# Latent attention: rope scores with 128 rows, against rope keys kept twice and padded with zeros

## The chip, the core and the metric

The kernel runs on one core of a Trainium2 chip. The metric is the device time of one execution, in microseconds (us). The engines of the core are TensorE (PE for its matmuls, PEld for its weight loads), VectorE (DVE), ScalarE (ACT), GpSimd (POOL) and SyncE (SP), which issues most of the loads. Each works through its own queue in order and waits on semaphores for the others.

## What is computed

The reference chains two blocks over 256 tokens of 1024 features. The first has stick-breaking attention, attention to a memory and a feed-forward net; the second has a layer with latent attention and a layer with a long convolution (Hyena), each followed by a convolved feed-forward net. The change concerns the latent attention alone:

```
def mla_mixer(x, cos, sin, w_in, g_q, w_uq, g_kv, w_ukv, w_o):
    h = x @ w_in
    c_q, c_kv, k_rope = jnp.split(h, [Q_LORA_RANK, Q_LORA_RANK + KV_LORA_RANK], axis=-1)
    q = (rms_norm(c_q, g_q) @ w_uq).reshape(b, s, MLA_HEADS, QK_NOPE_DIM + QK_ROPE_DIM)
    q_nope = q[..., :QK_NOPE_DIM]
    q_rope = apply_rope(q[..., QK_NOPE_DIM:], cos[:, :, None], sin[:, :, None])
    k_rope = apply_rope(k_rope, cos, sin)
    ...
        sc = (jnp.einsum('bqhd,bkhd->bhqk', qn, k_nope)
              + jnp.einsum('bqhr,bkr->bhqk', qr, k_rope))
        p = jax.nn.softmax(sc.astype(jnp.float32) * scale, axis=-1).astype(v.dtype)
        return jnp.einsum('bhqk,bkhd->bqhd', p, v)
```

There are 8 heads. A head's query and key have 128 features without position ("nope") and 64 with rotary position ("rope"). The rope key is one for all heads.

## The kernel before

Activations are kept with features on the partitions (rows) and the 256 tokens along the free dimension. Each fp32 product is made of three matmuls of split operands: a high part and a low part, hi x hi, lo x hi, hi x lo (`mm3`, lines 106 to 109; `gemm_b` at L102 for projections). A split is a copy on ACT (L69) and a subtract on DVE (L70). Weights come through a raw tile (`wraw`) and are split into `whi` and `wlo`.

The latent attention goes like this. `c_mm` and `first_pair` give the compressed queries, keys and the rope key (in rows 0 to 63 and once more in rows 64 to 127, since the host repeats its columns). `qr` matmuls give the rope queries, two heads on the 128 rows of a tile: four tiles of `rope_in`, and the rope key as the fifth. GpSimd's queue copies `rope_in` with its halves swapped to `rope_sw`. `rotate(i)` multiplies by the cosine and sine tables, adds, and splits tile i into `rope_h` and `rope_l`.

Eight `Latent` heads then run through `pipeline`: `scores`, `turn`, `values`, each head a step behind the one before, with the projections of head h + 2 (`mla_proj`: `qn`, `kn`), further rotations and the first output products (`u_wo`, tile `acc`) as fillers. For each of two blocks of 128 queries, `scores` makes three matmuls over the 128 nope rows and three over the 64 rope rows of its head (`r`: rows 0 to 63 for an even head, 64 to 127 for an odd one), all into one PSUM bank `z`. Heads 0 to 4 take the two banks `z300` and `z301` in turn, so head 2 has to wait until head 0's exponentials are read; the others take `z3` banks of the common pool. Then DVE takes the row maximum (`sm_nm`, L262), ACT the exponentials (`sm_p`, L270), DVE the reciprocal and the scaling (L273, L275); PE transposes (`pt`, L282), ACT copies (`sm_pt`, L284), PE multiplies with the values (`o`, L733), and the result is split into `oT`.

The order on each engine is set by the tile framework's scheduler, not by the text: it takes instructions of different heads as its own estimates let them come ready. Buffers (three of each of `qn` and `kn`, three raw tiles, five split pairs) set when loads and splits can go ahead.

Of the kernel before, what the change touches and what calls it, by code (L numbers as in the profile page):

```python
# [9 lines left out]
F32 = mybir.dt.float32  # L10
F32R = mybir.dt.float32r
# [7 lines left out]
P = 128  # L19
S = 256  # L20
# [25 lines left out]
def block_kernel(ctx, tc, A, out, taps=None):  # L46
    nc = tc.nc
# [10 lines left out]
    def bank(name="ps"):  # L58
        return psp.tile([P, 512], F32, name=name, tag="ps")

    def acc_bank(b, h, name="acc"):
        return accp.tile([P, 512], F32, name=f"{name}{b}{h}", tag=f"acc{b}{h}")
# [5 lines left out]
    def split(hi, lo, src, eng=nc.vector):  # L68
        nc.scalar.activation(hi, src, AF.Copy)  # L69
        eng.tensor_tensor(lo, src, hi.bitcast(F32), op=ALU.subtract)  # L70
# [34 lines left out]
    def mm3(ps, a, m, start, stop):  # L105
        (ah, al), (mh, ml) = a, m
        nc.tensor.matmul(ps, ah, mh, start=start, stop=False)  # L107
        nc.tensor.matmul(ps, al, mh, start=False, stop=False)  # L108
        nc.tensor.matmul(ps, ah, ml, start=False, stop=stop)  # L109
# [149 lines left out]
    def softmax(pool, z, scale, scale_ap):  # L259
        z = z.rearrange("p (b s) -> p b s", b=2)  # L260
        nm = small.tile([P, 2], F32, name="sm_nm", tag="sm_nm")
        nc.vector.tensor_reduce(nm, z, axis=AX.X, op=ALU.max, negate=True)  # L262
        if scale_ap is None:
            nc.vector.tensor_scalar(nm, nm, scale, None, op0=ALU.mult)
        else:
            nc.vector.tensor_tensor(nm, nm, scale_ap, op=ALU.mult)
        p = pool.tile([P, 2, S], F32, name="sm_p", tag="sm_p", bufs=2)
        sm = small.tile([P, 2], F32, name="sm_s", tag="sm_s")
        for b in range(2):
            nc.scalar.activation(p[:, b, :], z[:, b, :], AF.Exp, bias=nm[:, b:b + 1],  # L270
                                 scale=scale if scale_ap is None else scale_ap[:, b:b + 1],
                                 accum_out=sm[:, b:b + 1])
        nc.vector.reciprocal(sm, sm)  # L273
        for b in range(2):
            nc.vector.tensor_scalar(p[:, b, :], p[:, b, :], sm[:, b:b + 1], None, op0=ALU.mult)  # L275
        return p
# [42 lines left out]
    for k in range(KT):  # L319
# [3 lines left out]
        for b in range(2):  # L323
            tb = slice(b * P, (b + 1) * P)
# [75 lines left out]
    class Stick:  # L400
# [5 lines left out]
        def scores(self):  # L406
            q, k = qk["q", self.pair], keys[self.pair % 2]
            late, early = acc_bank(0, 0, "z"), acc_bank(0, 1, "z")
            mm3(early[:, :S], [t[:, :P] for t in q], [t[:, :, :P] for t in k], True, True)
            mm3(late, [t[:, P:] for t in q], [t for t in k], True, True)  # L410
            ze = early[:, :S].rearrange("p (h s) -> p h s", h=2)
            zl = late.rearrange("p (h g s) -> p h g s", h=2, g=2)
            stay = stays[self.pair % 2]
            w = p1.tile([P, 2, 3, P], F32, name="sb_w", tag="sb_w", bufs=2)
            for t, sc in ((stay, -0.125), (w, 0.125)):
                nc.scalar.activation(t[:, :, 0, :P], ze, AF.Sigmoid, scale=sc)
                nc.scalar.activation(t[:, :, 1:, :P], zl, AF.Sigmoid, scale=sc)
            later = p1.tile([P, 2, 3, 129], F32, name="sb_later", tag="sb_later", bufs=2)
            flat = [t.rearrange("p h g s -> p (h g s)")[:, ::-1] for t in (later, stay, reset)]
            nc.vector.tensor_tensor_scan(flat[0], flat[1], flat[2], 0.0, op0=ALU.mult, op1=ALU.max)  # L420
            nc.vector.tensor_tensor(w, w, later[:, :, :, 1:], op=ALU.mult)
            self.w = w
# [174 lines left out]
    p3 = ph.enter_context(tc.tile_pool(name="p3", bufs=1))  # L597
# [6 lines left out]
    sq = p3.tile([P, S], F32, name="sq")  # L604
    rope_in = p3.tile([P, 5, S], F32, name="rope_in")
    rope_sw = p3.tile([P, 5, S], F32, name="rope_sw")
    rope_h = p3.tile([P, 5, S], F32R, name="rope_h")
    rope_l = p3.tile([P, 5, S], F32R, name="rope_l")

    def c_mm(nt):  # L610
        w = weights(A["mla_w_in"][nt - 4])
# [22 lines left out]
    def rms_scales():  # L634

        for b in range(2):
            for dst, cs in ((rkv, slice(384, 512)), (rq, slice(0, 384))):
                junk = p3.tile([P, 384], F32, name="junk", tag="junk", bufs=2)
                nc.scalar.activation(junk[:, :cs.stop - cs.start], utok[:, b, cs], AF.Square,
                                     accum_out=dst[:, b:b + 1])  # L640
        ps = bank("ss")
        for b in range(2):
            nc.tensor.matmul(ps[:, b:b + 1], sq[:, b * P:(b + 1) * P], ones, start=True, stop=True)
        nc.vector.tensor_tensor(rkv, rkv, ps[:, :2], op=ALU.add)
        for dst, n in ((rkv, 256), (rq, 384)):
            nc.vector.tensor_scalar(dst, dst, 1.0 / n, RMS_EPS, op0=ALU.mult, op1=ALU.add)
            nc.gpsimd.tensor_tensor(dst, dst, mhalf, op=ALU.pow)
        nc.vector.tensor_scalar(rq, rq, 192.0 ** -0.5, None, op0=ALU.mult)
# [3 lines left out]
    for i in range(2):  # L652
        w = weights(A["w_uq_r"][i])
        for j in range(2):
            ps = bank("qr")
            gemm_b(ps[:, :S], w, j * 384, cq, 3)
            nc.scalar.activation(rope_in[:, 2 * i + j, :], ps[:, :S], AF.Copy)
    rms_scales()
    for q in range(4):
        s0 = (q ^ 1) * 32  # L660
# [40 lines left out]
    def rotate(i):  # L701
        nc.vector.tensor_tensor(rope_in[:, i, :], rope_in[:, i, :], cosT, op=ALU.mult)
        nc.vector.tensor_tensor(rope_sw[:, i, :], rope_sw[:, i, :], sinT, op=ALU.mult)
        nc.vector.tensor_tensor(rope_in[:, i, :], rope_in[:, i, :], rope_sw[:, i, :], op=ALU.add)
        split(rope_h[:, i, :], rope_l[:, i, :], rope_in[:, i, :])

    rotate(4)
    rotate(0)

    class Latent:  # L710
# [2 lines left out]

        def scores(self):
            h = self.h
            r = slice(64 * (h % 2), 64 * (h % 2) + 64)
            z = acc_bank(0, h % 2, "z3") if self.own else bank("z3")
            for b in range(2):
                tb = slice(b * P, (b + 1) * P)
                zb = z[:, b * S:(b + 1) * S]  # L720
                mm3(zb, [t[:, tb] for t in qn[h]], kn[h], True, False)
                mm3(zb, [t[r, h // 2, tb] for t in (rope_h, rope_l)],
                    [t[r, 4, :] for t in (rope_h, rope_l)], False, True)
            self.p = softmax(p3, z, None, rq)

        def turn(self):
# [17 lines left out]
    for i in range(1, 4):  # L744
        filler[2 * i - 2].append((rotate, i))
# [448 lines left out]
```

## Time and profile before

| | us |
|---|---|
| median of three runs | 989.87 |
| the three runs | 989.59, 989.87, 994.86 |
| profiled execution | 988.41 |
| its span, first to last instruction | 986.6 |
| busy: PE, PEld, DVE, ACT, POOL | 946.4, 841.1, 760.4, 524.5, 123.3 |

A span of 986.6 us in an execution of 988.41 leaves 1.8 us around it. Matmuls are listed with their fill and drain, so that neighbours overlap: how fast PE goes is seen from the distance between two starts, not from a duration. "64*128" behind a matmul is its form on the array, rows by columns; "128*128" is the whole. A row of the timeline gathers neighbours of one kind (x3), and its duration runs to the end of the last. In brackets stands the idle time before it and who ended it.

### The profile page before, as it was taken

How to read it: one execution, taken by the hardware profiler on the slowest of the kernel's cores; microseconds unless marked ns; L12 is line 12 of the kernel's file. 1: busy time of each engine (PE TensorE's matmuls, PEld its weight loads, DVE VectorE, ACT ScalarE, POOL GpSimd, SP SyncE). 2: the span in 40 equal slices, each digit the busy share in tenths (PEclk: the TensorE clock that was granted, in tenths of full speed). 3: DMA queues.
4: the chain of work that ended last, by engine and by line, in shares of the span. 5: the costliest groups of instructions: out<-in, count | busy, mean ns of one | idle time of the engine just before them, and what ended most of it. 6: DMA issues, size and time to landing. Idle time of an engine off the chain costs nothing.

```text
span 986.6 us, 15543 instructions
## 1 busy us (share of the span) xinstructions
PE 946.4 (96%) x6020; PEld 841.1 (85%) x6020; DVE 760.4 (77%) x1177; ACT 524.5 (53%) x859; POOL 123.3 (12%) x78
## 2 busy tenths in 40 slices
PE   9999999999999999999999999998879899999996
PEld 7889789888998888888899999788867789999995
DVE  6776678666557777779889887869998778777776
ACT  5676526445445576556666665345453346555551
POOL 0000000000000110011311211177453000000000
PEclk9999999999999999999999999999999899999999
DMA  7744436656565543466545556443222455555551
GB/s 242 278 170 129 154 122 221 178 190 179 183 192 187 173 128 107 149 244 210 196 164 184 171 170 220 132 160 106 98 86 86 171 192 193 179 185 185 181 191 43
DMA packets 48921, 165.97 MB, mean 168 GB/s; under 512 B 5995, under 2 KB 6860, under 8 KB 48720
## 3 DMA queue, kind: packets, MB, share of 16 engines
q1 hardware_dynamic: 48656, 164.34, 50.5%
q8 instruction: 47, 0.77, 0.3%
q0 software_dynamic: 192, 0.66, 0.2%
q14 instruction: 26, 0.21, 0.1%
HBM read 163.27 MB, written 1.05 MB: 167 GB/s over the span
## 4 chain that ended last, share of the span: by engine, by line
PE 76%; DVE 13%; DMA 5%; ACT 3%; issue 2%; POOL 0%; SPq 0%; DVEq 0%; ACTq 0%
PE up L102 30%; PE acc L108 8%; PE acc L107 8%; PE acc L109 8%; PE f L189 5%; PE proj L102 2%; DVE wlo L70 2%; PE z L107 1%; DMA wraw<-w_qk 1%; DVE yl L70 1%; DVE spec_q L956 1%; ACT whi L69 1%; DVE spec_q L955 1%; PE qn L102 1%; DMA wraw<-w_v 1%
## 5 line engine op out<-in xcount | busy, mean ns | idle before, releaser
L70 DVE TENSOR_TENSOR wlo<-wraw,whi 128x1024 fp32r<-128x1024 f32 (+1 forms) x246 | 300.6, 1225 | 71.2 <-ACT whi L69 70.9
L69 ACT ACTIVATE whi<-wraw 128x1024 fp32r<-128x1024 f32 (+1 forms) x270 | 281.0, 1045 | 113.3 <-PE acc L108 54.3
L102 PE MATMUL up<-xh,whi 128*128 128x256 f32 x864 | 122.0, 283 | 1.3 <-DVE t L763 1.3
L102 PEld LDWEIGHTS up<-xh,whi 128*128 128x128 f32 x864 | 115.3, 191 | 8.3 <-ACT whi L69 1.6
L102 PE MATMUL up<-xh,wlo 128*128 128x256 f32 x864 | 121.3, 283 | 0.0
L102 PE MATMUL up<-xl,whi 128*128 128x256 f32 x864 | 121.3, 283 | 0.0
L108 PE MATMUL acc<-whi,hl 128*128 128x512 f32 x304 | 119.6, 394 | 1.5 <-DVE hl L70 1.5
L109 PE MATMUL acc<-wlo,hh 128*128 128x512 f32 x304 | 119.6, 395 | 0.0
L107 PE MATMUL acc<-whi,hh 128*128 128x512 f32 x304 | 119.3, 394 | 0.0
L102 PEld LDWEIGHTS up<-xl,whi 128*128 128x128 f32 x864 | 111.5, 192 | 0.0
L102 PEld LDWEIGHTS up<-xh,wlo 128*128 128x128 f32 x864 | 111.4, 192 | 0.0
L156 POOL TENSOR_TENSOR ln_rs<-ln_rs,mhalf 128x1 f32<-128x1 f32 x12 | 11.7, 971 | 629.1 <-DVE ln_rs L155 629.1
L760 ACT ACTIVATE t<-up,wc 128x256 f32<-128x256 f32 x80 | 37.8, 474 | 94.8 <-PE up L102 94.7
L761 DVE SCALAR_TENSOR_TENSOR t<-up,wc,t 128x255 f32<-128x255 f32 x80 | 38.2, 479 | 51.4 <-ACT t L760 51.3
L108 PEld LDWEIGHTS acc<-whi,hl 128*128 128x128 f32 x304 | 57.1, 188 | 12.9 <-DVE hl L70 2.5
L109 PEld LDWEIGHTS acc<-wlo,hh 128*128 128x128 f32 x304 | 57.1, 188 | 12.7
L107 PEld LDWEIGHTS acc<-whi,hh 128*128 128x128 f32 x304 | 57.6, 189 | 10.9 <-ACT hh L69 0.6
L70 POOL TENSOR_TENSOR wlo<-wraw,whi 128x1024 fp32r<-128x1024 f32 x24 | 59.5, 2497 | 54.8 <-ACT whi L69 54.7
L763 DVE SCALAR_TENSOR_TENSOR t<-up,wc,t 128x255 f32<-128x255 f32 x80 | 38.3, 480 | 2.1
L524 ACT ACTIVATE h<-up 128x256 f32<-128x256 f32 x28 | 10.8, 385 | 54.7 <-PE up L102 51.5
L525 DVE TENSOR_TENSOR h<-h 128x256 f32<-128x256 f32 x32 | 13.5, 424 | 27.0 <-ACT h L524 26.4
L829 POOL TENSOR_TENSOR Kf<-f_eo 128x512 f32<-128x512 f32 x16 | 23.0, 1460 | 63.5 <-ACT f_eo L826 63.5
(411 smaller groups left out, 1684.6 us busy)
## 6 DMA issues: line engine op xcount, KB each, us to landing
wraw<-ffn_w_up SPq DMA_DIRECT2D x80, 512.0 KB, 3.5
wraw<-ffn_w_down SPq DMA_DIRECT2D x44, 512.0 KB, 3.5
wraw<-w_down SPq DMA_DIRECT2D x32, 512.0 KB, 3.7
wraw<-w_up SPq DMA_DIRECT2D x28, 512.0 KB, 3.6
wraw<-hy_w_in SPq DMA_DIRECT2D x20, 512.0 KB, 3.3
wraw<-w_qk SPq DMA_DIRECT2D x14, 512.0 KB, 4.6
wraw<-w_out SPq DMA_DIRECT2D x8, 512.0 KB, 3.5
wraw<-mla_w_o SPq DMA_DIRECT2D x8, 512.0 KB, 3.3
```

The costliest lines, as they stand in the source:

```text
L69: nc.scalar.activation(hi, src, AF.Copy)
L70: eng.tensor_tensor(lo, src, hi.bitcast(F32), op=ALU.subtract)
L102: nc.tensor.matmul(ps, a[:, off + k * P:off + (k + 1) * P], m[:, k, :], start=i == 0, stop=i == len(seq) - 1)
L107: nc.tensor.matmul(ps, ah, mh, start=start, stop=False)
L108: nc.tensor.matmul(ps, al, mh, start=False, stop=False)
L109: nc.tensor.matmul(ps, ah, ml, start=False, stop=stop)
L189: nc.tensor.matmul(ps, x[xi][:, k, tb], ws[k // 2][wi][:, o:o + 512], start=i == 0, stop=i == len(seq) - 1)
L525: nc.vector.tensor_tensor(h, h, h, op=ALU.mult)
L760: norm["act"] = nc.scalar.activation(dst, ps, AF.Copy, scale=w3[:, 1:2])
L761: nc.vector.scalar_tensor_tensor(dst[:, 1:], ps[:, :S - 1], w3[:, 0:1], dst[:, 1:], op0=ALU.mult, op1=ALU.add)
L763: norm["dve"] = nc.vector.scalar_tensor_tensor(dst[:, :S - 1], ps[:, 1:S], w3[:, 2:3], dst[:, :S - 1], op0=ALU.mult, op1=ALU.add)
L829: nc.gpsimd.tensor_tensor(Kf[:, o, i, j, cs], eo[0], eo[1], op=op)
```

## The change

The five tiles of split rope rows become four (the queries), and the rope key gets tiles of its own, `krh` and `krl` (`kr`), of 128 x 2 x 256: in half 0 the key stands in rows 0 to 63 with zeros in rows 64 to 127, in half 1 the other way round. Four memsets write the zeros, at the start of the stage. For tile 4 `rotate` splits the rope key in two pieces of 64 rows. `scores` then multiplies all 128 rows of a query tile, which holds two heads, with the half that belongs to the head: the other head's rows meet zeros. `junk` has one buffer instead of two.

```
     rope_in = p3.tile([P, 5, S], F32, name="rope_in")
     rope_sw = p3.tile([P, 5, S], F32, name="rope_sw")
-    rope_h = p3.tile([P, 5, S], F32R, name="rope_h")
-    rope_l = p3.tile([P, 5, S], F32R, name="rope_l")
+    rope_h = p3.tile([P, 4, S], F32R, name="rope_h")
+    rope_l = p3.tile([P, 4, S], F32R, name="rope_l")
+
+    kr = [p3.tile([P, 2, S], F32R, name=f"kr{t}") for t in "hl"]
+    for t in kr:
+        nc.vector.memset(t[64:, 0, :].bitcast(F32), 0.0)
+        nc.vector.memset(t[:64, 1, :].bitcast(F32), 0.0)
...
-                junk = p3.tile([P, 384], F32, name="junk", tag="junk", bufs=2)
+                junk = p3.tile([P, 384], F32, name="junk", tag="junk")
...
-        split(rope_h[:, i, :], rope_l[:, i, :], rope_in[:, i, :])
+        if i < 4:
+            split(rope_h[:, i, :], rope_l[:, i, :], rope_in[:, i, :])
+            return
+        for j in range(2):
+            r = slice(64 * j, 64 * j + 64)
+            split(kr[0][r, j, :], kr[1][r, j, :], rope_in[r, i, :])
...
             h = self.h
-            r = slice(64 * (h % 2), 64 * (h % 2) + 64)
             z = acc_bank(0, h % 2, "z3") if self.own else bank("z3")
...
                 mm3(zb, [t[:, tb] for t in qn[h]], kn[h], True, False)
-                mm3(zb, [t[r, h // 2, tb] for t in (rope_h, rope_l)],
-                    [t[r, 4, :] for t in (rope_h, rope_l)], False, True)
+                mm3(zb, [t[:, h // 2, tb] for t in (rope_h, rope_l)], [t[:, h % 2, :] for t in kr], False, True)
```

The number of score matmuls stays. The scheduler also orders some work differently. On PE, between the scores of head 3 (`z_3915` before, `z_3923` now) and those of head 4 (`z_3996`, `z_4004`), stood the first five score matmuls of head 5 (`z_4060`, `z_4068`). Before:

```order
L109 MATMUL z_3915<-rope_l,rope_h 128x256
L107 MATMUL z_4060<-knh,qnh 128x256
L108 MATMUL z_4060<-knh,qnl 128x256
L109 MATMUL z_4060<-knl,qnh 128x256
L107 MATMUL z_4060<-rope_h 128x256
L108 MATMUL z_4060<-rope_h,rope_l 128x256
L107 MATMUL z_3996<-knh,qnh 128x256
```

Now, at the same place on PE:

```order
L109 MATMUL z_3923<-krl,rope_h 128x256
L107 MATMUL z_4068<-knh,qnh 128x256
L107 MATMUL z_4004<-knh,qnh 128x256
L108 MATMUL z_4004<-knh,qnl 128x256
L109 MATMUL z_4004<-knl,qnh 128x256
L107 MATMUL z_4004<-krh,rope_h 128x256
```

One of head 5's matmuls is left ahead of head 4's; the other four moved behind them. On DVE, at the start of the stage, stand the splits of weights (`wlo`), the scales of the queries (`rq`) and the low parts of the compressed vectors (`cl`). Before:

```order
L70 TENSOR_TENSOR wlo<-wraw,whi 128x768 x2
L646 TENSOR_SCALAR rq<-rq 128x2
L648 TENSOR_SCALAR rq<-rq 128x2
L70 TENSOR_TENSOR wlo<-wraw,whi 128x768
L619 SCALAR_TENSOR_TENSOR cl<-c,gqk,ch 128x256
```

Now, at the same place on DVE:

```order
L70 TENSOR_TENSOR wlo<-wraw,whi 128x768 x2
L612 MEMSET krh 64x256
L613 MEMSET krh 64x256
L612 MEMSET krl 64x256
L613 MEMSET krl 64x256
L70 TENSOR_TENSOR wlo<-wraw,whi 128x768
L651 TENSOR_SCALAR rq<-rq 128x2
L653 TENSOR_SCALAR rq<-rq 128x2
L624 SCALAR_TENSOR_TENSOR cl<-c,gqk,ch 128x256
```

The memsets stand behind the second split of 768 columns, and the third such split moved ahead of the two operations on rq.

## Rows read from the trace of the kernel before

**Rows 1.** The page, part 1: busy us (share of the span) x instructions.
```profile
PE 946.4 (96%) x6020; PEld 841.1 (85%) x6020; DVE 760.4 (77%) x1177; ACT 524.5 (53%) x859; POOL 123.3 (12%) x78
```
**Rows 2.** Busy by stretch: us; PE, PEld, DVE, ACT, POOL; clock, DMA share, GB/s.
```profile
358.50:391.20 32.70, 32.70 (x196) 26.00 (x195) 26.89 (x74) 22.72 (x58) 0.00 (x0) 1.00 0.23 81
391.20:416.00 24.80, 24.76 (x115) 19.93 (x115) 18.70 (x29) 14.21 (x21) 0.94 (x1) 1.00 0.51 171
```
**Rows 3.** Timeline, PE and PEld, head 1's scores: start us, us, instruction.
```profile
361.14 0.28 PE L108 MATMUL z<-knh,qnl 128*128 128x256 f32 x1
361.15 0.19 PEld L109 LDWEIGHTS z<-knl,qnh 128*128 128x128 f32 x1
361.26 0.27 PE L109 MATMUL z<-knl,qnh 128*128 128x256 f32 x1
361.46 0.18 PEld L107 LDWEIGHTS z<-rope_h 64*128 64x128 f32 x1
361.46 0.38 PE L107 MATMUL z<-rope_h 64*128 64x256 f32 x1
361.69 0.28 PE L108 MATMUL z<-rope_h,rope_l 64*128 64x256 f32 x1
361.81 0.28 PE L109 MATMUL z<-rope_l,rope_h 64*128 64x256 f32 x1
362.02 0.39 PE L102 MATMUL kn<-ch,whi 128*128 128x256 f32 x1
...
362.24 0.40 PE L102 MATMUL kn<-ch,wlo 128*128 128x256 f32 x2
```
**Rows 4.** Timeline, PE: projections in one form.
```profile
362.71 0.51 PE L102 MATMUL qn<-ch,whi 128*128 128x256 f32 x3
...
363.77 0.40 PE L102 MATMUL kn<-ch,whi 128*128 128x256 f32 x2
```
**Rows 5.** Timeline, PE: the first and the last run of 64 rows.
```profile
358.53 0.39 PE L107 MATMUL z<-rope_h 64*128 64x256 f32 x2
...
390.67 0.38 PE L107 MATMUL z<-rope_h 64*128 64x256 f32 x1
```
**Rows 6.** Timeline, ACT and PE: ahead of head 2's scores.
```profile
361.63 0.39 ACT L69 ACTIVATE qnh<-qn 128x256 fp32r<-128x256 f32 x1 [0.31 <-PE z L109]
362.04 1.28 ACT L270 ACT_TABLE_LOAD   x1
363.33 0.57 ACT L270 ACTIVATE sm_p<-z,sm_nm,rq 128x256 f32<-128x256 f32 x1
...
363.89 0.56 ACT L270 ACTIVATE sm_p<-z,sm_nm,rq 128x256 f32<-128x256 f32 x1
...
364.59 0.39 PE L107 MATMUL z<-knh,qnh 128*128 128x256 f32 x1
```
**Rows 7.** Timeline, PE and ACT: ahead of head 4's scores.
```profile
368.71 0.60 PE L733 MATMUL o<-sm_pt,v_mla 128*128 128x256 f32 x2
...
369.15 0.49 PE L282 MATMUL pt<-ident,sm_p 128*128 128x128 f32 x3
...
370.71 0.56 ACT L270 ACTIVATE sm_p<-z,sm_nm,rq 128x256 f32<-128x256 f32 x1
...
372.39 0.39 PE L107 MATMUL z<-knh,qnh 128*128 128x256 f32 x1
```
**Rows 8.** Timeline, PE and DVE; tiles kh and kl on DVE (ns min/median/max).
```profile
330.41 2.03 PE L189 MATMUL f<-f4h,xl 128*128 128x512 f32 x8
...
334.70 0.17 DVE L646 TENSOR_SCALAR rq<-rq 128x2 f32<-128x2 f32 x1 [3.08 <-ACT junk L639]
...
L349 DVE MEMSET kh<- x2: 272/272/272, 2.2 to 3.7; 64x256 f32 x2
...
L70 DVE TENSOR_TENSOR kl<-proj,kh x12: 407/419/429, 32.1 to 77.8; 64x256 fp32r<-64x256 f32 x12
```
**Rows 9.** Waits in 352 to 400: waiter <- waited for: us, times, longest.
```profile
DVE sm_nm L262 <- PE z L109: 4.6, 5, 1.4
```

## The prediction

> **What bounds the kernel now.** I read the page first: TensorE is busy for 946.4 of 986.6 us [rows 1], so what TensorE issues, and how closely, is what counts. The change touches one stage, the latent attention, so the second view is the table by stretches: in 358.5 to 391.2 us, where all the score matmuls with the rope rows lie, PE is busy for all 32.70 us at a granted clock of 1.00, DVE for 26.89 and ACT for 22.72 [rows 2]. A busy share of 100% hides gaps, because a matmul is listed with its fill and drain and overlaps the next. So the third view is the timeline of PE and of its weight loads: there the reader is to look at the distances between starts.
>
> Within one form the starts are even: nine 128x256 matmuls, from 362.71 to 363.77, are 1.06 us, 0.118 each [rows 4]. Around a change of form they are not [rows 3]. From knl (361.26, 128 rows) to the first rope matmul (361.46, 64 rows) is 0.20, to the next 0.23, then 0.12 again; from the last rope matmul (361.81) to the next full one (362.02) is 0.21, and to the one behind it 0.22. From 361.26 to 362.24 are five steps, 0.98 us, where five even steps would take 0.59: 0.39 too much for two changes of form, **0.195 us for each**. The load column says why: inside a form the weights are loaded a step ahead (361.15 for the matmul of 361.26), at a change the load starts together with its own matmul (361.46 and 361.46).
>
> **The change part by part.**
>
> *Removed: the changes of form.* All 48 rope matmuls get 128 rows, so every matmul of the stage has the same form. Runs of 64-row matmuls between full ones: 19, the first at 358.53, the last at 390.67 [rows 5], thus 38 changes. 38 x 0.195 = 7.4 us on PE, which is the path here.
>
> *Lost: matmuls side by side.* The first row of rows 5 is two rope matmuls of heads 0 and 1 in 0.39 us, where one alone takes 0.38: they stand in different halves of the rows and start together. There are four such pairs, each saving a step of 0.118; with 128 rows they queue. Price 4 x 0.118 = 0.5 us. Ceiling: 7.4 - 0.5 = **6.9 us**.
>
> The length of a matmul stays: 256 columns, listed with 0.28, or 0.38 to 0.39 behind a change, in both forms [rows 3].
>
> *Added on DVE: four memsets of 64x256*, 0.272 us each [rows 8], 1.1 us. In the new order they stand behind the second 768-wide weight split. There DVE is idle for 3.08 us, up to 334.70 [rows 8]. The first waits for the last f matmul (the reuse of the second block's buffers), which is in the row of 330.41, 2.03 long, so until about 332.5; the four then end by 333.7. Behind them are queued a weight split, rq and the cl that the qr matmuls read; nothing of it is late. I take 0; without that cover it is 1.1 us. One junk buffer in place of two: the four squares are ACT work, in order on ACT already; 0, at most the 0.3 us of a late ch.
>
> *Added: one split more.* The rope keys are split in two halves, each 64x256. Such a subtract takes 0.419 us on DVE, like a 128-row one [rows 8], and ACT's copy I bound by the 0.39 of a 128x256 copy [rows 6]. The two copies stand ahead of the copy rope_h of the first head pair, for which the first rope matmul waits. From 0 to 0.3 us later; I take 0.15.
>
> *New waits on PE.* The softmax chains on ACT and DVE do not get shorter, and PE now comes to them sooner. Two I can work out.
> (a) The scores of head 2 go into head 0's bank and wait until its exponentials are read. That chain starts at the last nope matmul of head 1 (361.26, done 361.53), which frees the buffer for a copy of qn at 361.63; then come the table load (1.28) and two exponentials, and PE goes on at 364.59 [rows 6]: 3.33 us after the start of that matmul. PE's way from it to the scores of head 2 is three rope, eleven kn and nine qn matmuls, in both orders: 24 even steps, 24 x 0.118 = 2.83. So it waits 0.50 there; now it waits 0.11 (the matmul before starts at 363.77 + 5 x 0.118 = 364.36). New: 0.4.
> (b) The scores of head 4 wait in the same way for head 2's exponentials. From the last transpose of head 1 (369.15 + 2 x 0.11 = 369.37) to the end of those exponentials (370.71 + 0.56) is 1.90, with the hand-over of 0.14 seen at 364.59 it is 2.04. In the new order PE has behind that transpose itself 0.11, two o matmuls of 0.44 each (one o instruction is listed as two records, the x2 of 368.71, and the next instruction starts at 369.15) and eight steps of 0.118: 1.9 to 2.0. New wait: about 0.1. Before, PE came 1.1 us after them (372.39 against 371.27) [rows 7], and the order had four z matmuls more ahead of it: that slack is used up.
> The other heads have the same gates; with the slack of (b) as a guide I take 0.3 for all six, between 0 and 2.
>
> Sum: 6.9 - 0.15 - 0.4 - 0.1 - 0.3 = **6.0 us**. Behind the stage everything is released by work, so it moves up as a whole: in 391.2 to 416 the next matmuls follow at PE 24.76 of 24.80 [rows 2], and DVE has there 6 us of idle time for splits that slip. SP's and POOL's orders are unchanged.
>
> A rule that speaks against this: the Trainium skill, "TensorE: Matmul & The Clock Gate", Part 3, "The mechanism", says that a weight load for row groups that do not conflict, or for the background buffer, is pulled ahead of running matmuls. By it the load at a change of form would be hidden and the change would win nothing; the rows show it late at both edges, and I go by them.
>
> **The rivals.**
>
> *DVE takes over.* 26.89 us of DVE work lie in a stretch that is to shrink to 26 [rows 2], and 4.6 us of DVE's waiting is for the last z matmul of a head before its maximum [rows 9]. If the splits of weights in that stretch cannot slip behind it and half of that waiting stays, it takes 26.9 + 0.4 + 2.3 = 29.6, and 3.1 us are won: 985.3 against the profiled run, 986.8 against the median. For it: DVE is at 82%. Against it: part of the 26.9 are splits of weights, which the order places there for later use, and only the heads' chains must be on time.
>
> *The gap is not the form's.* If PE pauses whenever the operands' kind changes (rope after nope), it pauses still. Then nothing is won; the side by side pairs cost 0.5, and the added split 0.15 to 0.3: slower, by 0.8, **989.2** against the profiled run and 990.7 against the median. It decides if the step from knl to a rope matmul stays at 0.20. Against it: inside 362.02 to 364.36 qn and kn, with other weights and other banks, alternate without a pause [rows 4]. The rule of the page above would end at the same time.
>
> *More is won.* No new waits, the pairs' loss aside: 6.9, so 981.5 against the profiled run.
>
> **How the numbers follow.** The profiled run took 988.41, the median of the three is 989.87; 988.4 - 6.0 = 982.4, and from the median 983.9. I take the middle, **983.2**. Chances: the forecast with its bounds (5 to 7.4 won, 981 to 984.9) 0.71; DVE takes over (1 to 5 won) 0.21; no gain or a loss 0.06; the rest, a shift of the later stages, 0.02. The range is 980.6 (7.4 and a run like the profiled one, a little less) to 987.2 (the DVE case against the median, a little more). About 0.5% is what a measurement of this kernel can tell from no change, so 4.9 us. Faster by more: 0.70 (nearly all of the forecast); within: 0.27; slower: 0.03.
>
> **What would show it.** Right: in the timeline of PE all z matmuls at 128*128 and 0.12 apart, also from knl to the rope one; 358.5 to the last z about 26 to 27 us long; a wait of PE for sm_p ahead of head 2's scores of about 0.5; the memsets inside an idle time of DVE before 334. Wrong: steps of 0.2 left at the rope matmuls (second rival), or waits of PE for DVE sm_p, knl or oTl that add up to more than 2 us (first rival), or memsets followed by a late cl and qr.

## The result, and the profile after

The changed kernel took 986.84 us (median of 20 runs, 980.78 to 989.91) against 992.25 us for the kernel before in the same comparison: a ratio of 0.9947, 95% interval 0.9933 to 0.9962, so 5.3 us less. Two later comparisons of the same two kernels gave 0.9973 (0.9955 to 0.9992) and 0.9966 (0.9949 to 0.9984). The three, weighted by their intervals, come to 0.996, about 4 us. The profiled execution took 985.69 us, its span is 983.8.

What the page and the table by stretches say now (part 1: busy us, share of the span, instructions; then the stretch of [rows 2]):

```profile
PE 942.8 (96%) x6020; PEld 841.7 (86%) x6020; DVE 762.1 (77%) x1182; ACT 524.4 (53%) x860; POOL 123.9 (13%) x78
...
358.50:391.20 32.70, 32.16 (x223) 28.82 (x222) 30.33 (x81) 25.13 (x63) 0.00 (x0) 1.00 0.25 81
```

The same 32.70 us hold 223 matmuls in place of 196, still at a clock of 1.00, and DVE and ACT do more in them. PE is no longer listed busy all the time: there are short waits now, where pauses had been.

The timeline of PE and PEld in the scores of heads 0 and 1, close to the place of [rows 3] (start us, us, instruction):

```profile
361.07 0.28 PE L109 MATMUL z<-knl,qnh 128*128 128x256 f32 x1
361.07 0.19 PEld L107 LDWEIGHTS z<-krh,rope_h 128*128 128x128 f32 x1
361.19 0.28 PE L107 MATMUL z<-krh,rope_h 128*128 128x256 f32 x1
361.31 0.27 PE L108 MATMUL z<-krh,rope_l 128*128 128x256 f32 x1
```

From knl to the first rope matmul is 0.12, where it was 0.20, and the rope weights load at 361.07, a step ahead of their matmul at 361.19. It is so at 44 of the 48 rope matmuls; of the others the first waits for ACT (below), and three are listed 0.03 us behind a transpose or an `o`.

How long the stage is shows best between two of PE's instructions that bound it in every kernel, the first qr matmul and the first transpose of the normalization behind it. Timeline of PE, the kernel before and then the changed one:

```profile
338.89 0.83 PE L102 MATMUL qr<-ch,whi 128*128 128x256 f32 x3
...
414.07 1.27 PE L169 MATMUL ln_t<-ident,xt 128*128 128x128 f32 x8
```

```profile
340.19 0.62 PE L102 MATMUL qr<-ch,whi 128*128 128x256 f32 x3 [0.76 <-ACT sq L634]
...
410.34 0.66 PE L169 MATMUL ln_t<-ident,xt 128*128 128x128 f32 x4
```

75.2 us became 70.1: **5.0 us**. But qr itself started late, with a wait of 0.76 that the kernel before does not have. This leaves two questions: whether the 5 us are the changes of form, and what that wait is.

### The profile page after: what moved, and what is told of

Same layout as the page of the kernel before. It is cut to its first block, busy times and chain, and to the rows that moved or that the text cites. A ratio compares the mean times of both kernels' runs of the same rounds, so it can differ in the third digit from the quotient of the medians.

```text
span 983.8 us, 15550 instructions
## 1 busy us (share of the span) xinstructions
PE 942.8 (96%) x6020; PEld 841.7 (86%) x6020; DVE 762.1 (77%) x1182; ACT 524.4 (53%) x860; POOL 123.9 (13%) x78
## 4 chain that ended last, share of the span: by engine, by line
PE 72%; DVE 15%; DMA 6%; ACT 4%; issue 3%; POOL 1%; SPq 0%; DVEq 0%; ACTq 0%
PE up L102 30%; PE acc L108 8%; PE acc L107 8%; PE acc L109 8%; PE f L189 5%; PE proj L102 2%; DVE wlo L70 2%; ACT whi L69 1%; DMA wraw<-w_qk 1%; DVE yl L70 1%; DVE spec_q L963 1%; DVE spec_q L964 1%; DVE spec_w L966 1%; DMA wraw<-w_v 1%; DMA wraw<-ffn_w_up_f 1%
## 5 line engine op out<-in xcount | busy, mean ns | idle before, releaser
L837 POOL TENSOR_TENSOR Kf<-f_eo 128x512 f32<-128x512 f32 x16 | 23.1, 1462 | 63.5 <-ACT f_eo L834 63.5
```

Of the source, the lines that this page charges most:

```text
L837: nc.gpsimd.tensor_tensor(Kf[:, o, i, j, cs], eo[0], eo[1], op=op)
```

## The experiments

In each profile two sums were formed over PE's starts from the first score matmul to the last: the distance to the next start, less the even distance inside a form (0.118 for a 256-column matmul, 0.2335 for 512 columns, 0.109 for a transpose, 0.2185 for each of an o's two records), once for the steps at and right behind a change of form, once for all others (these are waits). The stage is the distance from qr to the transpose.

| kernel | runs of 64 rows | changes seen | paused at them | other waits | stage | ratio, 95% interval |
|---|---|---|---|---|---|---|
| before | 19 | 37 | 6.6 | 0.4 | 75.2 | 1 |
| form64 | 18 | 35 | 6.8 | 0.7 | 76.2 | 1.0026 (1.0004 to 1.0047) |
| grouped_before | 12 | 24 | 4.4 | 1.2 | 73.8 | 0.9976 (0.9958 to 0.9995) |
| even128 | 10 | 19 | 3.9 | 1.7 | 74.0 | 0.9992 (0.9971 to 1.0014) |
| changed, three times | 0 | 0 | 0 | 2.1, 2.2, 2.2 | 70.1, 70.3, 70.8 | 0.9947, 0.9973, 0.9966 |
| alt_after | 0 | 0 | 0 | 2.2 | 70.0 | 0.9989 (0.9972 to 1.0006) |

**Is it the form?** First the form alone was undone.

```diff
+            r = slice(64 * (h % 2), 64 * (h % 2) + 64)
...
-                mm3(zb, [t[:, h // 2, tb] for t in (rope_h, rope_l)], [t[:, h % 2, :] for t in kr], False, True)
+                mm3(zb, [t[r, h // 2, tb] for t in (rope_h, rope_l)], [t[r, h % 2, :] for t in kr], False, True)
```

> The changed kernel, in which only the scores read 64 rows again (of the query tile and of the padded key); memsets, added split and single junk buffer stay. PE's order then has 18 runs of 64-row matmuls. Theory (the change of form costs PE 0.195 us): 36 changes x 0.195 = 7.0 us come back, so from the first score matmul to the last 38 to 39 us as against 33.6 with 128 rows, and the time is that of the kernel before or a little above, 0 to +2 us, ratio 1.000 to 1.002. Rival (the gain came from the other order on PE or from tiles of its own for the key): it stays near 34 us and at a ratio of 0.995.

Everything came back, and 1.0 us on top of it (76.2 against 75.2). From the first score matmul to the last it is 38.9 us, as expected; the ratio of 1.0026 is a little above the expected 1.000 to 1.002, and its interval reaches into them. Timeline of PE and PEld in head 1's scores of form64:

```profile
361.39 0.28 PE L109 MATMUL z<-knl,qnh 128*128 128x256 f32 x1
361.60 0.18 PEld L107 LDWEIGHTS z<-krh,rope_h 64*128 64x128 f32 x1
361.60 0.38 PE L107 MATMUL z<-krh,rope_h 64*128 64x256 f32 x1
361.82 0.28 PE L108 MATMUL z<-krh,rope_l 64*128 64x256 f32 x1
...
362.14 0.39 PE L102 MATMUL kn<-ch,whi 128*128 128x256 f32 x1
```

The tiles and the order on PE are the changed kernel's, the distances those of before: 0.21 from knl to the first rope matmul, 0.22 to the next, and the load again starts with its matmul. The new tiles and the new order have no part in the gain.

**Is it in proportion?** Two kernels with fewer runs (10 and 12), reached in different ways: even128 keeps 64 rows for the odd heads; grouped_before has no zeros at all and only puts the rope matmuls of a head's two query blocks side by side.

```diff
-                mm3(zb, [t[:, h // 2, tb] for t in (rope_h, rope_l)], [t[:, h % 2, :] for t in kr], False, True)
+                r = slice(64 * (h % 2), P)
+                mm3(zb, [t[r, h // 2, tb] for t in (rope_h, rope_l)], [t[r, h % 2, :] for t in kr], False, True)
```

> The changed kernel, in which only the even heads use 128 rows; the odd heads read rows 64 to 127. PE's order has 10 runs of 64-row matmuls. Theory (price per change of form): 20 x 0.195 = 3.9 us more on PE than with 128 rows everywhere, so 37 to 37.5 us from the first score matmul to the last if no wait shrinks, 36 to 37 if those for the softmax do; 2 to 3 us faster than the kernel before, ratio 0.997 to 0.998. Rival (waits for ACT and DVE set the end, not PE's steps): within 1 us of the 33.6.

```diff
-                mm3(zb, [t[:, tb] for t in qn[h]], kn[h], True, False)
+                if b == 0:
+                    mm3(zb, [t[:, tb] for t in qn[h]], kn[h], True, False)
                 mm3(zb, [t[r, h // 2, tb] for t in (rope_h, rope_l)],
-                    [t[r, 4, :] for t in (rope_h, rope_l)], False, True)
+                    [t[r, 4, :] for t in (rope_h, rope_l)], b == 1, b == 0)
+                if b == 1:
+                    mm3(zb, [t[:, tb] for t in qn[h]], kn[h], False, True)
```

> The kernel before, in which the second block's rope matmuls come ahead of its nope ones, so that the rope matmuls of a head's two blocks stand next to each other: 12 runs of 64 rows in place of 19, with no zeros, no added memset and no added split. Theory (0.195 us per change of form): 24 x 0.195 = 4.7 us of pauses for the form in place of 7.1, so 2.4 us less: from the first qr matmul to the first transpose behind the stage 72.8 us (75.2 before, 70.2 with 128 rows everywhere); ratio 0.997 to 0.998. Rival (what was won came with the padded key, its tiles or the added DVE work): 75 us, ratio 1.000.

The price held: 0.20 and 0.185 per change. The stage did not shrink in full proportion (73.8 in place of 72.8 for grouped_before; for even128 1.2 us less than before, where 2 to 3 were expected in the time), because waits grew. The largest on PE, in grouped_before ahead of head 2's scores, in even128 ahead of the first rope matmul:

```profile
365.43 0.39 PE L107 MATMUL z<-knh,qnh 128*128 128x256 f32 x1 [0.71 <-ACT sm_p L270]
```

```profile
360.39 0.69 PE L107 MATMUL z<-krh,rope_h 128*128 128x256 f32 x2 [0.60 <-ACT rope_h L69]
```

The table shows the same from kernel to kernel: with fewer pauses (6.6, 4.4, 3.9, 0) the other waits rise (0.4, 1.2, 1.7, 2.1). A quarter to a half of what the form gives back goes into them. The timed ratio of grouped_before (2.4 us won) is as expected. That of even128, 0.9992, is above the expected 0.997 to 0.998, and its interval holds both these and no gain at all.

**The form, or the kind of operand?** Nope and rope matmuls were put in turn, in both kernels: the same matmuls and the same number.

```diff
...
+        seq = [m for pair in zip(*ms) for m in pair]
+        for i, (a, m) in enumerate(seq):
+            nc.tensor.matmul(ps, a, m, start=i == 0, stop=i == 5)
...
```

> The kernel before, in which each block's six score matmuls go nope, rope, nope, rope, nope, rope instead of three and three: the same matmuls, but 47 runs of 64 rows in place of 19. Theory (0.195 us per change of form): 94 x 0.195 = 18.3 us of pauses in place of 7.1, so about 11 us more: 48 to 49 us from the first score matmul to the last (37.9 before), ratio 1.010 to 1.012. Rival (the next weights are loaded ahead at a change too, and the pauses had another reason): within 1 us of the kernel before.

> The changed kernel with the same order, nope and rope in turn, all at 128 rows. Theory (only the form counts): no pause more, 33 to 34.5 us from the first score matmul to the last, ratio 0.994 to 0.997. Rival (PE pauses when the kind of operand changes, or when other weights follow in one accumulation): as many pauses as the 64-row kernel in this order, 47 to 49 us, ratio about 1.01.

With 128 rows the order costs nothing in the stage (70.0 us, waits 2.2). Timeline of PE in alt_after:

```profile
361.31 0.28 PE L726 MATMUL z<-krl,rope_h 128*128 128x256 f32 x1
361.42 0.28 PE L726 MATMUL z<-krh,rope_l 128*128 128x256 f32 x1
361.54 0.28 PE L726 MATMUL z<-knl,qnh 128*128 128x256 f32 x1
```

Its ratio of 0.9989 was expected lower (0.994 to 0.997), and the stage doesn't explain it; its executions had a mean granted clock of 0.980, those of the kernel before 0.983 in the same comparison; the last section takes this up. With 64 rows the same order cost far more than expected, 26 us in place of 11. Timeline of PE in alt_before, an early and a later place, then its table by stretches (us; PE, PEld, DVE, ACT, POOL; clock, DMA share, GB/s):

```profile
360.55 0.38 PE L716 MATMUL z<-knh,qnh 128*128 128x256 f32 x1
360.86 0.38 PE L716 MATMUL z<-rope_h 64*128 64x256 f32 x1
361.17 0.38 PE L716 MATMUL z<-knh,qnl 128*128 128x256 f32 x1
...
384.19 0.58 PE L716 MATMUL z<-rope_h,rope_l 64*128 64x256 f32 x1
384.70 0.58 PE L716 MATMUL z<-knl,qnh 128*128 128x256 f32 x1
```

```profile
358.00:362.60 4.60, 4.60 (x19) 2.79 (x17) 2.12 (x8) 2.25 (x6) 0.00 (x0) 1.00 0.00 0
362.60:369.40 6.80, 6.80 (x22) 5.04 (x23) 3.85 (x12) 3.65 (x10) 0.00 (x0) 0.50 0.00 1
...
383.20:400.20 17.00, 17.00 (x50) 12.23 (x50) 5.79 (x16) 5.67 (x16) 0.00 (x0) 0.50 0.09 31
```

At the full clock a step is 0.31, the even 0.118 and one change of 0.195, as the theory has it. From 362.6 to 369.4, behind such steps, and in four later stretches, the clock is granted at 0.50 (1.2 GHz, the lower of its two levels), and a step takes 0.51; between them it is back at 1.00. These stretches are 34 of the stage's 100.7 us. An estimate from the two steps: 34 x (1 - 0.31/0.51) is about 13 us, which with the expected 11 makes most of the 26. So the expected price is shown, and the rest is the clock, which neither theory had.

**The wait ahead of qr.** ACT and PE in the first profile of the changed kernel, and in its second:

```profile
333.65 0.84 ACT L69 ACTIVATE whi<-wraw 128x768 fp32r<-128x768 f32 x1
...
337.35 0.47 ACT L623 ACTIVATE ch<-c,gqk 128x256 fp32r<-128x256 f32 x1 [1.28 <-DMA gqk<-mla_g]
...
339.74 0.40 ACT L634 ACTIVATE sq<-c 128x256 f32<-128x256 f32 x1
```

```profile
336.64 0.48 ACT L623 ACTIVATE ch<-c,gqk 128x256 fp32r<-128x256 f32 x1 [0.32 <-DMA gqk<-mla_g]
...
339.11 0.39 ACT L634 ACTIVATE sq<-c 128x256 f32<-128x256 f32 x1
339.55 0.63 PE L102 MATMUL qr<-ch,whi 128*128 128x256 f32 x3
```

gqk is a load of 2.5 KB. From its issue to its last packet it took 4.1 us in the first profile (the ch that waits for it starts 0.4 later), 3.1 and 2.8 in the next two of the same kernel, 1.5 to 3.3 in the other kernels that load it at this place. Only in the first did PE wait. But the change has its part: before, sq ended 0.9 us ahead of the last c matmul's start; now it ends 0.1 behind it even when gqk is on time. The scheduler had put a weight split of 0.84 (333.65) between the squares on ACT, after which the next square starts 0.73 later than without it, and with one junk buffer in place of two the squares behind start 0.14 later each. So the squares end 1.0 us later. ACT's own way to the first ch is hardly longer for it (3.1 us from the start of the copy utok with gqk in place, 3.0 before), since that split had stood behind the squares. But DVE's rq waits for the squares, and the cl stand behind rq in DVE's order. Timeline of DVE in the first profile:

```profile
336.10 0.17 DVE L651 TENSOR_SCALAR rq<-rq 128x2 f32<-128x2 f32 x1 [0.63 <-ACT junk L644]
```

The third ch on ACT starts when the second cl is done, where gqk is on time 5.25 to 5.28 us from the start of utok, 4.67 before; and a fourth ch (0.36) now stands ahead of sq. Together that is 1.0 us, just what sq had spare.

> The changed kernel once more, beside the three below. Ratio 0.993 to 0.997; 33 to 34 us from the first score matmul to the last. In its first profile the scales gqk (a load of 2.5 KB) landed at about 337.3, 4.4 us after their issue, and the first ch on ACT, the copy sq and the first qr matmul came late by about 0.9 us; in the kernel before the load took 3.0 us at most. Theory (a matter of the execution, since its issue and what is queued ahead are the same): it lands within 3 us here. Rival (the change delays it): again over 4 us, and PE waits ahead of qr.

> The changed kernel, with gqk loaded at the start of the program into a tile that is kept. Theory (in the first profile of the changed kernel the wait of 0.76 ahead of qr was for this load): PE goes from the c matmuls to qr without a wait over 0.2 us, 0.8 to 0.9 us won against a run in which the load is late, nothing against one in which it is not. Rival (one junk buffer and the weight split moved between the squares delay ch): ch on ACT starts at the end of the last square and qr still waits for sq by 0.3 us or more. In the time 0 to 1 us against the changed kernel, too little for an interval.

```diff
+    gqk = const.tile([P, 5], F32, name="gqk")
...
+    nc.sync.dma_start(gqk, A["mla_g"])
...
-    gqk = p3.tile([P, 5], F32, name="gqk")
-    nc.sync.dma_start(gqk, A["mla_g"])
```

In after_again the load took 3.1 us, PE did not wait ahead of qr, and the ratio of 0.9973 came out just above the expected 0.997. In gqk_early, with gqk there from the start, the first ch follows the last square at once, and PE goes from c to qr with no wait; sq still ends 0.1 behind the last c matmul's start. Timeline of ACT:

```profile
334.65 0.18 ACT L644 ACTIVATION_READ_ACCUMULATOR junk<-utok 128x1 f32 x1
334.74 0.46 ACT L623 ACTIVATE ch<-c,gqk 128x256 fp32r<-128x256 f32 x1
...
336.88 0.84 ACT L623 ACTIVATE ch<-f4t,gqk 128x256 fp32r<-128x256 f32 x2 [0.37 <-DVE cl L624]
337.61 0.39 ACT L634 ACTIVATE sq<-c 128x256 f32<-128x256 f32 x1
```

The ratio was 0.9959 (0.9941 to 0.9978) beside 0.9973 for the changed kernel in the same comparison: on the expected side, too near to be told apart.

**The wait ahead of head 2's scores.** exp_early brings ACT's table load ahead of the scores; gqk_exp has both edits.

```diff
+    warm_e = p3.tile([P, 1], F32, name="warm_e")
+    nc.scalar.activation(warm_e, mhalf[:, :1], AF.Exp)
```

> The changed kernel, with one exponential of a single column ahead of the rotations, so that the table load of 1.28 us lies before the scores and not ahead of head 0's exponentials. Theory (head 2's scores wait for head 0's exponentials, 0.52 and 0.11 us after that): that wait is gone, the pauses on PE from the first score matmul to the last fall from 2.1 to about 1.5 us, 33.0 in place of 33.6. Rival (DVE's maxima or the copies of qn are as late): another wait of 0.3 us or more stands in its place, the sum stays within 0.2 of 2.1.

> Both of these edits on the changed kernel. Sum of the two if they are independent: 0.6 to 1.5 us faster than the changed kernel, ratio to the kernel before 0.992 to 0.996.

The wait of 0.52 went, as its theory said, and the sum did not, as its rival said: 2.5 us of waits in exp_early (more than the rival's 2.3) and 2.0 in gqk_exp, against 2.1 to 2.2. In both, new waits of 0.1 to 0.26 stand between 372 and 374.5 us, ahead of an `o` and the scores behind it, and in exp_early the first rope matmul waited 0.4 longer:

```profile
359.89 0.51 PE L107 MATMUL z<-krh,rope_h 128*128 128x256 f32 x2 [0.58 <-ACT rope_h L69]
```

The stage took 70.2 and 69.7, the ratios are 0.9969 (0.9949 to 0.9989) and 0.9953 (0.9935 to 0.9971): no gain that can be told from the changed kernel's.

**Once more, and elsewhere.**

> The changed kernel a third time, since its first two comparisons (0.9947 and 0.9973) lie at each other's bounds. If the stage is all that differs, 4.9 us of 990: 0.995; if something behind the stage is lost as well, 0.997. In the profile 70.1 to 70.4 us from the first qr matmul to the first transpose behind the stage, and a wait ahead of qr only if gqk takes over 3.2 us to land.

It came in between (0.9966), with 70.8 us of stage, above the expected 70.4, and no wait ahead of qr. mem128 gives the four memory heads of the first block the same form, best adds gqk_exp to it. The two padded key tiles `mks` and their memsets are left out here:

```diff
...
+            nc.scalar.activation(mks[i % 2][r, hh, :], ps[r, :S], AF.Copy)
...
-                nc.tensor.matmul(z[:, b * S:(b + 1) * S], q[r, b * P:(b + 1) * P], k[r, :],
+                nc.tensor.matmul(z[:, b * S:(b + 1) * S], q[:, b * P:(b + 1) * P], k[:, self.hh, :],
```

> The changed kernel with the same idea in the first block: the four heads that attend to the memory read all 128 rows of their queries, against memory keys kept twice with zeros. Theory: four runs of 64 rows (from 85 to 109 us) cost a pause of 0.2 at either end, 4 x 0.39 = 1.6 us, and as the added memsets are DVE's at the start and the added copies ACT's, 1.2 to 1.6 us are won on PE there; ratio 0.0012 to 0.0016 below the changed kernel's. Rival (the copies in halves, or the softmax of these heads, set the end there): the stretch from 84 to 122 us keeps its length within 0.3.

> The changed kernel with the early gqk, the early exponential and the 128 rows for the memory heads: the sum of what these gave, 1.5 to 2.5 us below the changed kernel, ratio to the kernel before 0.992 to 0.995.

In the profile mem128 won 0.8 us over the stretch of these heads, which in the changed kernel is 72 to 109 us, where 1.2 to 1.6 were expected. (It was 2.9 us late at the start of this stretch, behind a later load of weights and with a granted clock of 0.62 from 72 to 76 us; so its profiled time says nothing of the gain.) Timeline of PE around one of the four runs, the changed kernel first and then mem128:

```profile
93.06 0.60 PE L439 MATMUL pv<-sb_wt,v_sb 128*64 128x256 f32 x6
93.59 1.13 PE L454 MATMUL mz<-mk,mq 64*128 64x256 f32 x4
94.65 0.75 PE L102 MATMUL proj<-f4h,whi 128*128 128x256 f32 x4
```

```profile
95.83 0.60 PE L449 MATMUL pv<-sb_wt,v_sb 128*64 128x256 f32 x6
96.36 1.13 PE L463 MATMUL mz<-mk,mq 128*128 128x256 f32 x4
97.14 1.05 PE L102 MATMUL proj<-f4h,whi 128*128 128x256 f32 x6
```

The step out of the run got shorter (from mz to proj 1.06, now 0.78, of which part moved to the step behind); the step into it did not (0.53 from pv to mz both times), because the matmul ahead has half the columns, 128*64, and 128*64 to 128*128 is a change of form too. The expectation had counted both ends. The ratios are 0.9948 (0.9928 to 0.9968) for mem128 and 0.9941 (0.9921 to 0.9961) for best, beside 0.9966 for the changed kernel in the same comparison. best has the lowest ratio of all, within the expected 0.992 to 0.995; the intervals overlap, so that it beats the changed kernel is likely and not shown.

## Why the prediction was right

*What bounds, and the price of a change.* Right. The price of 0.195 was read from five steps at one place. form64, even128 and grouped_before give 0.19, 0.20 and 0.185 over 35, 19 and 24 changes, the early part of alt_before 0.195. With side by side pairs counted in, the kernel before paused 6.6 us at 37 changes, where the sum had 6.9. The Trainium skill, "TensorEngine Tiling (Array Packing)", "Key Properties", says that changing the tiling mode drains TensorE; the traces show a pause at each change and give its price, and do not show whether the engine is empty in it.

*The length of a matmul.* Right: 0.28, 0.12 apart, in either form.

*Memsets.* Right in place and price. Timeline of DVE in the changed kernel:

```profile
332.94 0.27 DVE L612 MEMSET krh<- 64x256 f32 x1 [0.49 <-PE f L189]
...
334.03 0.27 DVE L613 MEMSET krl<- 64x256 f32 x1
334.52 0.96 DVE L70 TENSOR_TENSOR wlo<-wraw,whi 128x768 fp32r<-128x768 f32 x1 [0.22 <-ACT whi L69]
```

They wait for the last f matmul, end at 334.30, and the split behind them waits for ACT, not for them. That nothing behind them is late was wrong for rq, by 1.0 us, and through it for the cl; the squares on ACT are the cause, not the memsets.

*One junk buffer.* Here a step was too small: 0 to 0.3 us of a late ch. The working looked at DVE's order at this place and not at ACT's, where a weight split had moved between the squares. The split and the single buffer together cost nothing by themselves, but take 1.0 us of cover away, and the first profile shows the price without that cover, 0.9.

*The added split.* 0.15 was taken, 0.3 the bound; PE waits 0.34 more than an even step and 0.10 in the step behind. The bound counted ACT's two copies. What came late is on DVE, ACT and PE:

```profile
358.08 0.86 DVE L70 TENSOR_TENSOR krl<-rope_in,krh 64x256 fp32r<-64x256 f32 x2
358.97 0.43 DVE L709 TENSOR_TENSOR rope_in<-rope_in,rope_sw 128x256 f32<-128x256 f32 x1
359.43 0.42 ACT L69 ACTIVATE rope_h<-rope_in 128x256 fp32r<-128x256 f32 x1
359.90 0.50 PE L107 MATMUL z<-krh,rope_h 128*128 128x256 f32 x2 [0.18 <-ACT rope_h L69]
```

The two subtracts stand ahead of the addition for the first queries, whose copy PE waits for; the second of them is the added one.

*The two waits worked out.* (a) The matmul of head 2 comes 0.52 late, with 0.11 behind it; before it was 0.11 and 0.10. New: 0.4, predicted 0.4. (b) Head 4: 0.14 and 0.11, predicted 0.1 (its matmul is the second in the row of 370.19).

```profile
365.35 0.39 PE L107 MATMUL z<-knh,qnh 128*128 128x256 f32 x1 [0.36 <-ACT sm_p L270]
365.57 0.28 PE L108 MATMUL z<-knh,qnl 128*128 128x256 f32 x1
...
370.19 0.64 PE L107 MATMUL z<-knh,qnh 128*128 128x256 f32 x2
370.67 0.28 PE L108 MATMUL z<-knh,qnl 128*128 128x256 f32 x1
```

One thing was left out of all of them: a wait also costs 0.10 to 0.11 in the step behind it.

*The sum.* All waits together were taken as 0.95 and came to 2.1 - 0.4 = 1.7 us. So 6.6 - 1.7 = 4.9 us in place of 6.0, and the stage in the three profiles was 5.0, 4.8 and 4.4 shorter. The mechanism was right and the gain in the stage over by about a fifth, most of it in the term of the waits: the rope split 0.45 (0.15 taken), (a) 0.4 (0.4), (b) 0.25 (0.1), the other heads 0.6 (0.3). From the first rope matmul to the last score matmul it is 28.1 us (32.5 before), where 26 to 27 were named as a sign of being right.

*The number.* 983.2 was forecast and 986.84 measured; 3.1 of these 3.6 us are the kernel before itself, for which the forecast took the middle of 988.4 and 989.9 and which had 992.25 in the comparison. That the gain agreed is in part luck: the 5.3 us of the first comparison lie just inside the forecast's 5 to 7.4 and just above the 4.9 taken as the least that can be told, the 4 us of the mean of three lie below both.

*The rivals.* That the gap is not the form's is refuted by form64 and alt_after. DVE did not take over, although the 986.8 us of this rival are the measured time almost to the digit. It came near: it is busy for 30.3 of 32.7 us, and its wait for the last score matmul of a head, 4.6 us in [rows 9], is down to this:

```profile
DVE sm_nm L262 <- PE z L109: 0.7, 1, 0.7
```

PE's remaining waits are for ACT, mostly.

*Behind the stage.* That nothing slips there holds up to the transpose: from the last score matmul to it are 22.4 to 23.1 us in the three profiles, 23.1 before. But the whole time moved less (4 us in the mean of three comparisons) than the stage (4.4 to 5.0). A late gqk explains up to 0.9 of that in an execution in which it happens. The clock does not explain it on the mean: 17.4 us were lost to its lower level in 44 executions of the changed kernel, 17.2 in 86 of the kernel before. What takes the rest stays open.

## What to carry to other kernels

A busy share of 100% on TensorE can hide pauses, here 6.6 us in 32.7 us that are listed as wholly busy: look at the distances between starts, and count the changes of form (rows and columns) in its order, not the small matmuls. Each cost 0.195 us here, so padding with zeros paid, with runs of two or three 64-row matmuls on the mean and a matmul that takes as long with 128 rows. Grouping such runs gave a part of it in the stage with no added work (73.8 us, with zeros 70.8); in the time of the same comparison the two cannot be told apart (0.9976 and 0.9966). When the pauses go, the next chains show: here they took a quarter to a half of it back. Look at the queue of every engine at the places the change touches.

## What the runs showed of the hardware

With the alternating order the clock fell while PE was listed as busy without a gap: 1.00 from 358.0 to 362.6 us, then 0.50, with a pause of 0.195 us in each step of 0.31 before the fall. In the kernel before, with its 37 changes, the stage stays at 1.00, as it does in every other kernel here.

With the granted clock goes much of the scatter of one kernel's times. Over the 86 executions of the kernel before in the comparisons of the experiments, each us lost to the lower clock (the time, multiplied by what its mean granted clock lacks to 1.00) goes with 0.65 us more time (correlation 0.78), and the loss ranges from 12 to 25 us. Where it falls differs from one execution to the next; in two profiles, behind the stage (the kernel before, then the changed one; columns as in [rows 2]):

```profile
630.00:645.00 15.00, 12.79 (x59) 9.65 (x58) 9.82 (x15) 4.52 (x7) 3.46 (x3) 1.00 0.43 141
```

```profile
630.00:645.00 15.00, 12.70 (x63) 10.14 (x62) 5.72 (x10) 5.23 (x7) 5.51 (x4) 0.89 0.22 76
```

In the third profile of the changed kernel this stretch is at 1.00 again, so a fall there does not come with the change in every execution.

This accounts for alt_after's ratio. Its executions lost 19.7 us on the mean, those of the kernel before beside it 17.2. With 0.65 us taken off for each us lost, the means differ from the kernel before of the same comparison by 3.5 us less for alt_after, 3.5 and 3.8 less for the changed kernel (second and third comparison), 2.1 less for grouped_before, 1.2 less for even128 and 1.6 more for form64, each known to about 1 us. That is the order of the stages too. Why alt_after's executions lost more is not shown.
